# A second context tile leaves the dense second half of the expert layer: U dense, V by picked and fetched rows

## The chip, the cores and the metric

One core of a Trainium2 chip runs the whole program in one launch. The metric is the device time of one execution in microseconds (us); lower is better.

## The reference, cut to what matters

Two residual streams of 256 tokens, latents and context, pass through two layers (a mixer, then a PEER expert layer). Layer 0 mixes both streams; layer 1 needs the context only as keys and values of its mixer, after which the context is dropped.

```python
def peer_ffn(h, w_q, sub_keys, u, v):          # per 128 tokens
    q = (t @ w_q).reshape(PEER_CHUNK, PEER_HEADS, 2, PEER_KEY_HALF)
    s = jnp.einsum('thpk,hpnk->thpn', q, sub_keys)
    s_top, i_top = lax.top_k(s, PEER_TOPK)
...
    idx = jnp.take_along_axis(...)             # 8 heads x 16 = 128 experts of 16384 per token
    g = jax.nn.softmax(best_s, axis=-1)
    a = jnp.einsum('td,thkd->thk', t, u[idx])
    w = (jax.nn.gelu(a) * g)
    return jnp.einsum('thk,thkd->td', w, v[idx])
...
def odd_mixer(hl, hc, ...):                    # layer 1
    ql, kl, vl = jnp.split(hl @ w_in, ...)
    kc, vc = jnp.split(hc @ w_in[:, DIFF_QK_WIDTH:], [DIFF_QK_WIDTH], axis=-1)
    k_all, v_all = concat of latent and context
```

So each of four 128-token tiles in layer 0 (two of latents, two of context) picks 128 experts per token, and the context's result must be there before the keys and values of the context are projected in layer 1.

## The kernel before, in words

**Two ways through the expert layer.** The *dense* way multiplies a tile with all 16384 rows of U on TensorE (PE), applies GELU, multiplies by a gate table that is zero except at the tile's own 128 experts, and multiplies by all of V. Each product is three fp32r matmuls (high and low parts). The *gathered* way fetches, slot by slot, the one row per token (128 rows of 4 KB, an indirect DMA that POOL issues) and lets VectorE (DVE) do a dot product (`gather_u`) or a scaled add (`gather_v`). Both latent tiles and context tile 1 go the dense way in layer 0; context tile 0 is gathered. Layer 1 has two dense tiles (latents).

**Stages of layer 0.** Even mixer for both streams; `scores` and `route` of the context tiles, then of the latents (top-16 lists, all on DVE); `gate_table` for three tiles (DVE makes one-hots `goi`, `goj`; PE multiplies them; the table goes to DRAM). PE meanwhile runs `LEAD0` = 13 U steps ahead. Then `dense` (L600) loops 64 steps `c`: a U step (on average 1.5 units of 24 matmuls of 128x512, L634 to L636, operands `duh`, `dul`) and a V step (`w_prep`: DVE multiplies `dy` by the gates `dg`, L701, PE transposes it, L689; `v_mm`: 12 matmuls per tile, L708 to L710, operands `dvh`, `dvl`). The U steps are `LEAD0` ahead, so the last 13 steps have V alone.

**Then layer 1.** `ctx_ffn` (L885) writes the latents' norm first (`norm_T`, whose `rsqrt` is a chain of 13 small POOL instructions), then adds the context's results. `odd_mixer` (L914) projects Q of the latents (`oq`), norms the context into `oh`, and for each of 4 blocks projects K and V of both streams with one load of the weights, and runs 4 attention heads (`head`), which need K of both. `rotate` (L941) has one POOL instruction each. After the heads come the output projection, layer 1's expert layer and the final norm.

**What orders the work.** Program order and a scheduler fix a static order per engine; each engine takes its instructions in that order and waits at the head of its queue. POOL issues the indirect DMAs in the same queue in which its arithmetic stands. Row buffers (`row`, `ROWBUFS` = 4) live in the pool `vphase`, which exists only during the V steps: a fetch waits until DVE has used the row four places before.

Of the kernel before, what the change touches and what calls it, by code (L numbers as in the profile page):

```python
# [29 lines left out]
LEAD0 = 13  # L30
LEAD1 = 20
ROWBUFS = 4


def constants():
# [32 lines left out]
    c["iota"] = np.broadcast_to(np.concatenate([np.arange(128), STARTS, [1]]).astype(f32), (P, 145)).copy()  # L68
# [37 lines left out]
class Joined:  # L106
# [5 lines left out]
    def __getitem__(self, key):  # L112
        return (self.a if key[1] < 4 else self.b)[key]

# [23 lines left out]
class Builder:  # L138
# [59 lines left out]
    def setup(self, mods, *xp):  # L198
# [30 lines left out]
        self.iota, self.one = iota[:, 0:128], iota[:, 144:145]  # L229
# [236 lines left out]
    def route(self, sc, wk, ijg):  # L466
# [5 lines left out]
        va = wk.tile([P, 16, 16], F32, name="rv", bufs=2)  # L472
        ix = wk.tile([P, 16, 16], U32, name="rix", bufs=2)
# [63 lines left out]
    def gather_u(self, l, H, ijg, gp, wk):  # L537

        V, S = self.V, self.S
        idx = gp.tile([P, P], U32, name="gidx", bufs=1)  # L540
        V.scalar_tensor_tensor(idx, ijg[:, 0, :], 128.0, ijg[:, 1, :], op0=ALU.mult, op1=ALU.add)  # L541
        a = wk.tile([P, P], F32, name="pa", bufs=2)
# [5 lines left out]
        return idx  # L548

    def gather_v(self, l, idx, a, acc, gp):  # L550
        V = self.V
        for s in range(P):
            t = self.gather(gp, self.A[f"peer_v{l}"], idx, s)
# [12 lines left out]
    def gate_table(self, ijg, table, pool, ring):  # L566
# [10 lines left out]
        for t0 in range(0, P, 8):  # L577
            st = pool.tile([P, 8, P], F32, name="gst", bufs=2)
            for h in range(2):
# [12 lines left out]
                oj = pool.tile([P, 4, P], F32, name="goj", bufs=5)  # L592
# [7 lines left out]
    def dense(self, l, tables, hs, ups, yp, lead, mid, late, fin):  # L600
# [8 lines left out]
        nt = len(hs)  # L609
        uring = "c" if nt == 3 else "x"  # L610
# [18 lines left out]
        def u_unit(c, i):  # L629
            uh, ul = ut[c]  # L630
            hi, lo = hs[i]
            b = self.bank(uring)
# [9 lines left out]
        def u_step(c):  # L642
# [3 lines left out]
            for i in range((nt + 1) // 2) if c % 2 == 0 else range((nt + 1) // 2, nt):  # L646
                u_unit(c // 2, i)
# [6 lines left out]
        with self.pool("vphase") as vp:  # L654
            w = self.wide()
            pacc = [w[:, 0:512], w[:, 512:1024], self.bank("y"), self.bank("y")]
            if nt == 3:
                pacc = [self.bank("x"), self.bank("x")] + pacc[2:] + pacc[:2]
# [38 lines left out]
            def w_prep(c):  # L697
# [5 lines left out]
                if nt == 3:  # L703
                    ws[c].append(w_split("dx", lambda a: y[:, 2, a * P:(a + 1) * P], 2))
# [38 lines left out]
    def ffn(self, l, modT, h, wp, wclose, lead, extra=None, late=iter(()), finish=None):  # L743

        tables = [self.dr.tile([P, P * P], F32, name=f"table{l}{i}") for i in range(3 if extra else 2)]
        dense = [tuple(t[:, :, i * P:(i + 1) * P] for t in h) for i in range(2)]
        with self.pool("ypool") as yp:
# [7 lines left out]
            def mid():  # L755
                with self.pool("twork") as wk:
                    if extra:
                        self.gate_table(extra[1], tables[2], wk, "yx")
                    for r, table in zip(res, tables):
                        ijg = rw.tile([P, 3, P], F32, name="ijg", bufs=2)  # L760
                        self.route(r, rw, ijg)
                        self.gate_table(ijg, table, wk, "yx" if extra else "yc")
                dts.close()

            if extra:
                dense.append(extra[0])

            def fin(pacc, vp):
# [6 lines left out]
                if finish is not None:  # L775
                    finish(pacc[4:], vp)

            self.dense(l, tables, dense, ExitStack(), yp, lead, mid, late, fin)

    def run(self):  # L780
# [15 lines left out]
        with self.pool("emix") as mp, self.pool("tmp0") as self.tmp, self.pool("ework") as wk:  # L796
# [3 lines left out]
                        + [(mp, f"e{n}{s}", 1) for n in "qkvf" for s in range(2)])  # L800
# [7 lines left out]
            q, k, v, f = ([mp.tile([P, 2, 512] if n == "v" else [P, 4, 256], F32, name=f"e{n}{s}") for s in range(2)]  # L808
                          for n in "qkvf")
# [55 lines left out]
            tags = [(mp, f"e{n}{s}", 1) for n in "qkvf" for s in range(2)]  # L865
            with tc.issue_after(after):
                for m in range(3):
                    self.modulation(1, m, mod1, Tags((tags[1:] * 2)[m % 2:][:8]), "y", 1, Tags(tags[:1] * 2))
            sc1 = self.mod_scale(1, mod1, 0, 0)
            ijg1 = l0.tile([P, 3, P], F32, name="ijg1")  # L870
            self.route(sc_c[1], rw, ijg1)
# [163 lines left out]
```

## Time and profile before

| | |
|---|---|
| median of 3 runs | 2939.35 us (2938.17 to 2948.95) |
| profiled execution, its own time | 2946.36 us |
| its span on the profile | 2944.6 us |
| PE / DVE / ACT / POOL busy | 93% / 66% / 43% / 13% of the span |
| HBM traffic | 207 GB/s over the span |

The span is the time between the first and the last instruction on the profile; the execution's own time is 1.8 us more. A busy PE may still wait between stages, so the stages are read one by one. TensorE's granted clock is given as a share of its upper level (2.4 GHz).

### The profile page before, as it was taken

How to read it: one execution, taken by the hardware profiler on the slowest of the kernel's cores; microseconds unless marked ns; L12 is line 12 of the kernel's file. 1: busy time of each engine (PE TensorE's matmuls, PEld its weight loads, DVE VectorE, ACT ScalarE, POOL GpSimd, SP SyncE). 2: the span in 40 equal slices, each digit the busy share in tenths (PEclk: the TensorE clock that was granted, in tenths of full speed). 3: DMA queues.
4: the chain of work that ended last, by engine and by line, in shares of the span. 5: the costliest groups of instructions: out<-in, count | busy, mean ns of one | idle time of the engine just before them, and what ended most of it. 6: DMA issues, size and time to landing. Idle time of an engine off the chain costs nothing. (4 is left out here: it accounts for less than half of the span.)

```text
span 2944.6 us, 40707 instructions
## 1 busy us (share of the span) xinstructions
PE 2747.4 (93%) x14793; PEld 2272.7 (77%) x14793; DVE 1951.3 (66%) x3726; ACT 1266.8 (43%) x2220; POOL 391.7 (13%) x403
## 2 busy tenths in 40 slices
PE   6999987995999999999999989988898799999997
PEld 4776966885788888888788868787787688888886
DVE  3335799997778887888843445456898755555444
ACT  3334445575333333333332334344476444444443
POOL 0000000000345444545400001000000000000000
PEclk9998998997999999999999989999999899999999
DMA  6464464565989999999843423324466765666554
GB/s 244 127 221 93 157 228 133 167 182 155 360 299 340 345 342 330 343 331 329 314 157 120 155 71 125 127 65 151 155 192 202 239 234 197 212 213 208 168 158 136
DMA packets 297945, 612.83 MB, mean 208 GB/s; under 512 B 33664, under 2 KB 157328, under 8 KB 295184
## 3 DMA queue, kind: packets, MB, share of 16 engines
q1 hardware_dynamic: 260880, 475.99, 49.0%
q0 software_dynamic: 36864, 134.23, 12.4%
q8 instruction: 117, 1.92, 0.3%
q14 instruction: 84, 0.69, 0.1%
HBM read 565.04 MB, written 45.09 MB: 207 GB/s over the span
## 5 line engine op out<-in xcount | busy, mean ns | idle before, releaser
L681 DVE TENSOR_TENSOR dvl<-dv,dvh 128x1024 fp32r<-128x1024 f32 x256 | 305.4, 1221 | 231.3 <-ACT dvh L680 230.7
L634 PE MATMUL bank<-duh,h 128*128 128x512 f32 x1024 | 405.6, 399 | 7.9 <-ACT dy L640 4.8
L635 PE MATMUL bank<-dul,h 128*128 128x512 f32 x1024 | 408.0, 399 | 1.7 <-DVE dul L625 1.7
L636 PE MATMUL bank<-duh,h 128*128 128x512 f32 x1024 | 406.6, 398 | 0.0
L680 ACT ACTIVATE dvh<-dv 128x1024 fp32r<-128x1024 f32 x256 | 259.8, 1052 | 273.8 <-PE wide L710 163.6
L625 DVE TENSOR_TENSOR dul<-du,duh 128x1024 fp32r<-128x1024 f32 x256 | 310.2, 1220 | 93.5 <-ACT duh L623 92.2
L623 ACT ACTIVATE duh<-du 128x1024 fp32r<-128x1024 f32 x256 | 271.3, 1061 | 231.5 <-DMA du<-in_peer_uT 162.1
L709 PE MATMUL bank<-dvl,dwh 128*128 128x512 f32 x768 | 299.8, 391 | 0.0
L710 PE MATMUL bank<-dvh,dwl 128*128 128x512 f32 x768 | 294.2, 397 | 0.0
L708 PE MATMUL bank<-dvh,dwh 128*128 128x512 f32 x768 | 290.0, 396 | 0.0
L640 ACT ACTIVATE dy<-bank 128x256 f32<-128x256 f32 x320 | 105.0, 380 | 367.7 <-PE bank L636 349.7
L176 DVE TENSOR_TENSOR wl<-wt,wh 128x512 fp32r<-128x512 f32 x224 | 153.0, 689 | 138.0 <-ACT wh L175 136.5
L533 POOL DMA_INDIRECT row<-in_peer_u,gidx x128 | 170.4, 1331 | 551.2 <-DVE gidx L541 341.3
L634 PEld LDWEIGHTS bank<-duh,h 128*128 128x128 f32 x1024 | 193.5, 189 | 55.2 <-ACT dy L640 7.5
L635 PEld LDWEIGHTS bank<-dul,h 128*128 128x128 f32 x1024 | 193.9, 189 | 47.5 <-DVE dul L625 3.0
L636 PEld LDWEIGHTS bank<-duh,h 128*128 128x128 f32 x1024 | 193.6, 189 | 45.2
L596 PE MATMUL bank<-goj,goi 128*128 128x128 f32 x1280 | 174.1, 292 | 51.7 <-ACT goi L588 25.6
L175 ACT ACTIVATE wh<-wt 128x512 fp32r<-128x512 f32 x224 | 140.9, 631 | 183.9 <-PE bank L195 87.9
L596 PEld LDWEIGHTS bank<-goj,goi 128*128 128x128 f32 x1280 | 167.2, 205 | 63.1 <-ACT goi L588 31.5
L194 PE MATMUL bank<-h,wh 128*128 128x256 f32 x704 | 204.8, 292 | 7.1 <-ACT hf L326 6.3
L195 PE MATMUL bank<-h,wh 128*128 128x256 f32 x704 | 203.0, 289 | 1.1 <-DVE h L333 1.1
L196 PE MATMUL bank<-h,wl 128*128 128x256 f32 x704 | 202.4, 289 | 1.2 <-DVE wl L176 1.2
(261 smaller groups left out, 5655.2 us busy)
## 6 DMA issues: line engine op xcount, KB each, us to landing
du<-in_peer_uT SPq DMA_DIRECT2D x256, 512.0 KB
dv<-in_peer_v SPq DMA_DIRECT2D x256, 512.0 KB
table<-gst SPq DMA_DIRECT2D x80, 512.0 KB
dg<-table SPq DMA_DIRECT2D x320, 128.0 KB
wm<-in_w_mod SPq DMA_DIRECT2D x56, 512.0 KB
wt<-in_peer_w_q SPq DMA_DIRECT2D x96, 256.0 KB
wm<-in_w_mod SPq DMA_DIRECT2D x20, 1024.0 KB
wt<-in_odd_w_in SPq DMA_DIRECT2D x48, 256.0 KB
```

Source lines behind the costliest of these rows:

```text
L194: self.T.matmul(out, lhsT=a, rhs=b, start=k == 0 and m == 0, stop=False)
L596: T.matmul(b[:, t * P:(t + 1) * P], lhsT=oi[:, t, :], rhs=oj[:, t, :], start=True, stop=True)
L623: S.activation(th, t, AF.Copy)
L625: V.tensor_tensor(tl, t, th.bitcast(F32), ALU.subtract)
L634: T.matmul(b, lhsT=hi[:, k, :], rhs=uh[k], start=k == 0, stop=False)
L635: T.matmul(b, lhsT=hi[:, k, :], rhs=ul[k], start=False, stop=False)
L636: T.matmul(b, lhsT=lo[:, k, :], rhs=uh[k], start=False, stop=k == KT - 1)
L680: S.activation(th, v, AF.Copy)
L681: V.tensor_tensor(tl, v, th.bitcast(F32), ALU.subtract)
L708: T.matmul(b, lhsT=wh, rhs=v[0], start=first, stop=False)
L709: T.matmul(b, lhsT=wh, rhs=v[1], start=False, stop=False)
L710: T.matmul(b, lhsT=wl, rhs=v[0], start=False, stop=last)
```

## The change

- Context tile 1 keeps its dense U product, but GELU's result (`da`) goes to a DRAM table `ad` (128 tokens x 16384 experts). Its gate table, its V product and its transposes are gone.
- `pick_v`: for each of the 128 slots an indirect DMA fetches one number per token out of `ad` into a column of `pb` (a *pick*: 128 elements of 4 bytes). After every 16 picks DVE multiplies them with the gates, and 16 rows of V are fetched and added, as for tile 0.
- The experts' numbers (`gidx`) are made right after each context `route`, tile 0 first, and the row buffers live in the pool `lay0` from the even mixer on (they share their place with that mixer's context q, k, v, f). `gather_u` may so start during the routing of the other tiles.
- `LEAD0` is 16. Some buffers are smaller (`goj` 4, `rv`, `rix` 1, fewer places for the modulation's weights).
- `odd_mixer` projects Q, K and V of the latents first, with the modulations 3 and 4; then norms the context into the row buffers' place (`oh`), loads the K and V weights once more, and projects the context's K and V, with all heads in that second loop.

```diff
-LEAD0 = 13
+LEAD0 = 16
...
+    def pick_v(self, l, ad, ijg, idx, acc, gp):
...
+        flat = ad.rearrange("t (e o) -> (t e) o", o=1)
+        at = gp.tile([P, P], U32, name="gat")
+        V.tensor_scalar(at, idx, self.base, None, op0=ALU.add)
+        a = gp.tile([P, P], F32, name="pb")
         for s in range(P):
+            self.G.indirect_dma_start(out=a[:, s:s + 1], out_offset=None, in_=flat,
+                                      in_offset=bass.IndirectOffsetOnAxis(ap=at[:, s:s + 1], axis=0))
+            if s % PICK == PICK - 1:
+                c = slice(s + 1 - PICK, s + 1)
+                V.tensor_tensor(ijg[:, 2, c], a[:, c], ijg[:, 2, c], ALU.mult)
+                self.gather_v(l, idx, ijg[:, 2, :], acc, gp, range(s + 1 - PICK, s + 1))
...
+            if i == 2:
+                a = up.tile([P, UN], F32, name="da", bufs=2)
+                S.activation(a, b, AF.Gelu_apprx_tanh)
+                nc.sync.dma_start(ad[:, c * UN:(c + 1) * UN], a)
+                return
...
-                if nt == 3:
-                    ws[c].append(w_split("dx", lambda a: y[:, 2, a * P:(a + 1) * P], 2))
...
-        def ctx_ffn(pacc, vp):
+        def ctx_ffn():
             self.norm_T(1, sc1, "x", *hl)
-            self.add_ffn(1, pacc, gates[0], self.tmp.tile([P, D], F32, name="yctx"))
-            idx = self.gather_u(0, hc0, ijgc, vp, l0)
+            self.gather_u(0, hc0, ijgc, idx0, l0)
             acc = l0.tile([P, D], F32, name="gacc", tag="hc0")
-            self.gather_v(0, idx, ijgc[:, 2, :], acc, vp)
+            self.gather_v(0, idx0, ijgc[:, 2, :], acc, l0)
             self.add_ffn(0, (acc[:, :512], acc[:, 512:]), gates[0], acc)
+            acc = l0.tile([P, D], F32, name="gacc1", tag="h1c0")
+            self.pick_v(0, ad, ijg1, idx1, acc, l0)
+            self.add_ffn(1, (acc[:, :512], acc[:, 512:]), gates[0], acc)
...
         for c in range(4):
-            w = self.weight2(wp, w_in[4 + c])
-            self.project_T(kTs[1][:, c * 2:c * 2 + 2, :], w, hs[1], "x")
+            self.project_T(kTs[1][:, c * 2:c * 2 + 2, :], self.weight2(wp, w_in[4 + c]), hl, "x")
...
+            self.project(vs[1][:, :, c * 256:(c + 1) * 256], self.weight2(wp, w_in[8 + c]), hl, "x")
+            if 3 + c < 5:
+                self.modulation(1, 3 + c, modT, wk, "y", 4)
+
+        hc = [Halves(*(rows.tile([P, KT // 2, 256], F32R, name=f"oh{c}{i}", tag="row", bufs=ROWBUFS) for i in range(2)))
+              for c in range(2)]
+        self.norm_T(0, sc, "x", *hc)
+        for c in range(4):
+            self.project_T(kTs[0][:, c * 2:c * 2 + 2, :], self.weight2(wp, w_in[4 + c]), hc, "x")
+            self.project(vs[0][:, :, c * 256:(c + 1) * 256], self.weight2(wp, w_in[8 + c]), hc, "x")
```

**How the order moves.** In the changed program `gidx_4153` and `gacc` belong to context tile 0, `gidx_4343` and `gacc_13785` to context tile 1.

VectorE before, the end of the gate tables (`goi`, `goj` one-hots) and the first V step, whose first work is the multiply `dy`:

```order
L590 TENSOR_TENSOR goi<-c_iota,gsT 128x512
L593 TENSOR_TENSOR goj<-c_iota,gsT 128x512
L591 TENSOR_TENSOR goi<-goi,gsT 128x512 x3
L541 SCALAR_TENSOR_TENSOR gidx<-ijgc 128x128
L701 TENSOR_TENSOR dy<-dy,dg 128x768
L545 SCALAR_TENSOR_TENSOR row,pa<-row,hc_71 128x1024
L694 TENSOR_TENSOR dwl<-bank,dwh 128x512
```

VectorE in the changed program, first a piece of the latents' routing (`rs`, `rsm`, `rv`), then the rows around the first V step's `dy`:

```order
L458 MATCH_REPLACE rtmp<-rv,rs 128x128 x2
L524 TENSOR_TENSOR rs<-rpb,steps 128x2048
L563 SCALAR_TENSOR_TENSOR row,pa<-row,hc_71 128x1024
L542 RECIPROCAL rsm<-rsm 128x8
L563 SCALAR_TENSOR_TENSOR row,pa<-row,hc_71 128x1024
L459 MAX rv<-rtmp 128x8 x2
L563 SCALAR_TENSOR_TENSOR row,pa<-row,hc_71 128x1024
L656 TENSOR_TENSOR dul<-du,duh 128x1024
```

```order
L589 SCALAR_TENSOR_TENSOR gacc<-row,ijgc,gacc 128x1024
L623 TENSOR_TENSOR goi<-goi,gsT 128x512
L625 TENSOR_TENSOR goj<-c_iota,gsT 128x512
L623 TENSOR_TENSOR goi<-goi,gsT 128x512
L589 SCALAR_TENSOR_TENSOR gacc<-row,ijgc,gacc 128x1024 x8
L736 TENSOR_TENSOR dy<-dy,dg 128x512
L716 TENSOR_TENSOR dvl<-dv,dvh 128x1024
```

All 128 rows of `gather_u` (`row,pa`) and the first 17 of tile 0's `gather_v` (`gacc`) now stand ahead of the first `dy`; before, none did. Of the one-hots 160 stand ahead of it instead of 240, of the splits `dul` 41 instead of 29.

POOL before, tile 0's fetches and the start of the latents' norm for layer 1 (`ss`, `rs_t`, `rstd`):

```order
L533 DMA row<-in_peer_u,gidx 128x1024 x128
L533 DMA row<-in_peer_v,gidx 128x1024 x128
L312 TENSOR_SCALAR ss<-ss 128x2
L239 TENSOR_TENSOR rs_t<-rstd 128x2
L240 TENSOR_TENSOR rs_t<-rs_t,ss 128x2
L241 TENSOR_SCALAR rs_t<-rs_t 128x2
```

POOL in the changed program, from tile 0's fetches to the first picks (`pb`), and then a piece of the same norm:

```order
L548 DMA row<-in_peer_u,gidx_4153 128x1024 x128
L548 DMA row<-in_peer_v,gidx_4153 128x1024 x128
L548 DMA row<-in_peer_v,gidx_4343 128x1024 x4
L575 DMA pb<-ad,gat 128x1 x33
L548 DMA row<-in_peer_v,gidx_4343 128x1024 x2
L575 DMA pb<-ad,gat 128x1
L548 DMA row<-in_peer_v,gidx_4343 128x1024
L575 DMA pb<-ad,gat 128x1 x2
```

```order
L254 TENSOR_TENSOR rs_t<-rstd 128x2
L255 TENSOR_TENSOR rs_t<-rs_t,ss 128x2
L548 DMA row<-in_peer_v,gidx_4343 128x1024
L256 TENSOR_SCALAR rs_t<-rs_t 128x2
L257 TENSOR_TENSOR rstd<-rs_t,rstd 128x2
L548 DMA row<-in_peer_v,gidx_4343 128x1024 x11
L984 TENSOR_TENSOR oq<-oq,c_rope 128x256
L548 DMA row<-in_peer_v,gidx_4343 128x1024
L984 TENSOR_TENSOR oq<-oq,c_rope 128x256 x2
L548 DMA row<-in_peer_v,gidx_4343 128x1024
```

The 13 small instructions of the latents' norm are scattered among the picks: all 128 picks and 41 of tile 1's 128 rows stand ahead of the last of them (`rstd`). Another 46 rows stand between that and the last of the 16 rotations (`oq`, `ok`), and the last 41 behind those.

VectorE in the changed program, the end of tile 1's rows, among the splits `wl` of the weights:

```order
L191 TENSOR_TENSOR wl<-wt,wh 128x512
L589 SCALAR_TENSOR_TENSOR gacc_13785<-row,ijg_3964,gacc_13785 128x1024
L191 TENSOR_TENSOR wl<-wt,wh 128x512
L589 SCALAR_TENSOR_TENSOR gacc_13785<-row,ijg_3964,gacc_13785 128x1024 x38
L595 TENSOR_TENSOR gacc_13785<-gacc_13785,gate 128x512 x2
L596 TENSOR_TENSOR xl_12155<-xl_12155,gacc_13785 128x512 x2
L252 TENSOR_SCALAR rstd<-ss 128x2
L331 TENSOR_SCALAR xn<-xl_12153,rstd 128x1024
```

The last 38 rows stand together, with no other work between them; right behind them come the context's residual add and its norm. Before, no fetched row stood in this layer.

## Rows read from the trace of the kernel before

**Rows 1.** Busy time of each engine by stretch; columns as in its first line.
```profile
core 0: us, PE busy (x) PEld busy (x) DVE busy (x) ACT busy (x) POOL busy (x), PEclk, DMA share, GB/s
303.00:732.00 429.00, 362.96 (x2407) 317.29 (x2405) 399.04 (x1278) 237.56 (x493) 5.27 (x16) 0.94 0.53 168
732.00:1612.00 880.00, 874.03 (x3929) 711.19 (x3930) 644.59 (x751) 300.45 (x455) 347.75 (x254) 0.99 0.83 301
...
1790.00:1963.00 173.00, 170.95 (x1192) 141.79 (x1190) 84.47 (x189) 72.22 (x172) 6.28 (x8) 1.00 0.30 98
1963.00:2945.00 982.00, 910.23 (x4566) 756.54 (x4566) 617.02 (x1092) 471.60 (x738) 10.08 (x49) 0.96 0.58 187
```

**Rows 2.** PE's timeline (start, duration us): V steps without U, a projection.
```profile
1649.84 0.82 PE L689 MATMUL bank<-c_ident,dy 128*128 128x128 f32 x6
...
1658.69 0.82 PE L689 MATMUL bank<-c_ident,dy 128*128 128x128 f32 x6
...
1734.89 0.39 PE L708 MATMUL wide<-dvh,dxh 128*128 128x512 f32 x1
...
1737.39 0.39 PE L710 MATMUL wide<-dvh,dxl 128*128 128x512 f32 x1
...
1760.60 0.29 PE L195 MATMUL bank<-h,wh 128*128 128x256 f32 x1
1760.72 0.28 PE L196 MATMUL bank<-h,wl 128*128 128x256 f32 x1
```

**Rows 3.** DVE's timeline: neighbours, for the pace of each form.
```profile
600.55 1.21 DVE L625 TENSOR_TENSOR dul<-du,duh 128x1024 fp32r<-128x1024 f32 x1
601.69 0.68 DVE L591 TENSOR_TENSOR goi<-goi,gsT 128x512 f32<-128x512 f32 x1
602.29 0.28 DVE L478 CAST rixb<-rix 128x256 bf16<-128x256 uint32 x1
...
934.05 1.22 DVE L545 SCALAR_TENSOR_TENSOR row<-row,hc 128x1024 f32<-128x1024 f32 x1
935.20 0.08 DVE L545 DVE_READ_ACCUMULATOR row<-row,hc 128x1 f32 x1
...
1433.28 1.28 DVE L557 SCALAR_TENSOR_TENSOR gacc<-row,ijgc,gacc 128x1024 f32<-128x1024 f32 x1
1434.48 0.42 DVE L694 TENSOR_TENSOR dxl<-bank,dxh 128x256 fp32r<-128x256 f32 x1
```

**Rows 4.** Groups of POOL by form: count, busy us, mean ns, idle before.
```profile
L533 POOL DMA_INDIRECT row<-in_peer_v,gidx x128 | 179.8, 1405 | 174.6 <-DVE gacc L557 149.4 <-issue 12.5 <-DVE row L545 5.2
```

**Rows 5.** POOL's timeline: fetches back to back, a longer one, a norm's step.
```profile
730.35 0.94 POOL L533 DMA_INDIRECT row<-in_peer_u,gidx  x1 [0.31 <-issue]
731.59 0.94 POOL L533 DMA_INDIRECT row<-in_peer_u,gidx  x1 [0.31 <-issue]
...
1420.42 1.68 POOL L533 DMA_INDIRECT row<-in_peer_v,gidx  x1 [0.65 <-DVE gacc L557]
...
1749.49 0.19 POOL L242 TENSOR_TENSOR rstd<-rs_t,rstd 128x2 f32<-128x2 f32 x1
```

**Rows 6.** Timeline: two fetches (POOL), each with the use of its row (DVE).
```profile
1034.75 1.68 POOL L533 DMA_INDIRECT row<-in_peer_u,gidx  x1 [1.74 <-DVE row L545]
1044.35 1.23 DVE L545 SCALAR_TENSOR_TENSOR row<-row,hc 128x1024 f32<-128x1024 f32 x1 [3.61 <-DMA row<-in_peer_u,gidx]
1430.40 0.94 POOL L533 DMA_INDIRECT row<-in_peer_v,gidx  x1 [1.45 <-DVE gacc L557]
1435.35 1.29 DVE L557 SCALAR_TENSOR_TENSOR gacc<-row,ijgc,gacc 128x1024 f32<-128x1024 f32 x1 [0.45 <-DMA row<-in_peer_v,gidx]
```

**Rows 7.** Timeline after the last V matmul: last residual add, norm, first projection.
```profile
1742.48 1.28 DVE L564 TENSOR_TENSOR xl<-xl,yadd 128x512 f32<-128x512 f32 x2
1756.34 0.58 PE L194 MATMUL bank<-h,wh 128*128 128x256 f32 x1 [0.84 <-ACT hf L326]
```

**Rows 8.** Busy time of L270 (modulations) in the heads' stretch: PE, PEld.
```profile
1790.00:1963.00 173.00, 14.34 (x64) 2.25 (x64) 1.00 0.30 98
```

More of the change, by code (lines that the diff above doesn't have):

```diff
@@ L29 @@
 UN = 512
-LEAD0 = 13
+LEAD0 = 16
 LEAD1 = 20
 ROWBUFS = 4
+PICK = 16
 def constants():
@@ L113, in __getitem__, with __init__ @@
         return (self.a if key[1] < 4 else self.b)[key]
+class Halves:
+    def __init__(self, a, b):
+        self.a, self.b = a, b
+    def __getitem__(self, key):
+        p, k, n = key
+        if isinstance(k, slice):
+            return (self.a if k.start < 4 else self.b)[p, :, n]
+        return (self.a if k < 4 else self.b)[p, k % 4, n]
 class Slots:
@@ L535, in gather, with experts, gather_u @@
         return t
[L537 removed]
+    def experts(self, ijg, pool, name):
+        idx = pool.tile([P, P], U32, name=name)
+        self.V.scalar_tensor_tensor(idx, ijg[:, 0, :], 128.0, ijg[:, 1, :], op0=ALU.mult, op1=ALU.add)
+        return idx
+    def gather_u(self, l, H, ijg, idx, gp):
         V, S = self.V, self.S
[L540 to L542 removed]
+        a = gp.tile([P, P], F32, name="pa")
         for s in range(P):
@@ L645, in u_step @@
                 return
-            for i in range((nt + 1) // 2) if c % 2 == 0 else range((nt + 1) // 2, nt):
+            n = len(hs)
+            for i in range((n + 1) // 2) if c % 2 == 0 else range((n + 1) // 2, n):
                 u_unit(c // 2, i)
@@ L741, in dense, with ffn @@
             fin(pacc, vp)
-    def ffn(self, l, modT, h, wp, wclose, lead, extra=None, late=iter(()), finish=None):
-        tables = [self.dr.tile([P, P * P], F32, name=f"table{l}{i}") for i in range(3 if extra else 2)]
+    def ffn(self, l, modT, h, wp, wclose, lead, extra=None, late=iter(()), finish=None, ad=None):
+        tables = [self.dr.tile([P, P * P], F32, name=f"table{l}{i}") for i in range(2)]
         dense = [tuple(t[:, :, i * P:(i + 1) * P] for t in h) for i in range(2)]
@@ L775, in fin @@
                 if finish is not None:
-                    finish(pacc[4:], vp)
-            self.dense(l, tables, dense, ExitStack(), yp, lead, mid, late, fin)
+                    finish()
+            self.dense(l, tables, dense, ExitStack(), yp, lead, mid, late, fin, ad)
     def run(self):
@@ L799, in run @@
             tags = Tags([(p, f"h{c}", 1) for p in (hcp, self.pers) for c in range(2)]
-                        + [(mp, f"e{n}{s}", 1) for n in "qkvf" for s in range(2)])
+                        + [(l0, "row", ROWBUFS)] * 4 + [(mp, f"e{n}1", 1) for n in "qkvf"])
             mods = [self.mod_steps(0, m, mod0, tags, "c", 1, n=(4, 2)) for m in range(2)]
@@ L807, in run @@
             sc_mix = self.mod_scale(0, mod0, 0, 0)
-            q, k, v, f = ([mp.tile([P, 2, 512] if n == "v" else [P, 4, 256], F32, name=f"e{n}{s}") for s in range(2)]
-                          for n in "qkvf")
+            q, k, v, f = ([(mp if s else l0).tile([P, 2, 512] if n == "v" else [P, 4, 256], F32, name=f"e{n}{s}",
+                                                  tag=f"e{n}1" if s else "row", bufs=1 if s else ROWBUFS)
+                           for s in range(2)] for n in "qkvf")
             h = hc, hl = [[p.tile([P, KT, 256], F32R, name=f"h{c}") for c in range(2)] for p in (hcp, self.pers)]
@@ L912, in run, with odd_mixer @@
         right.close()
-    def odd_mixer(self, cp, mp, wk, wp, sc, modT, hl):
+    def odd_mixer(self, cp, mp, wk, wp, sc, modT, hl, rows):
         nc, A, V, S, G, T = self.nc, self.A, self.V, self.S, self.G, self.T
-        hs = [mp.tile([P, KT, 256], F32R, name=f"oh{c}") for c in range(2)], hl
         rope = self.const("rope", cp)
```

59 lines of the change are left out of this document (26 added, 33 removed).

## The prediction

> **What bounds the kernel now.** I read the busy times by stretch first, because the share of the whole span (PE 93%) hides stages with other limits. Four stretches matter [rows 1]. From 303 to 732 us (routing and gate tables) VectorE is busy 399 of 429 us and PE 363: VectorE sets this stretch. From 732 to 1612 us (U and V steps together) PE is busy 874 of 880 us, VectorE 645: PE sets it, and all 256 row fetches of context tile 0 lie here, hidden beside it. From 1790 to 1963 us (odd mixer's K, V and heads) PE is busy 171 of 173 us. The last 982 us are layer 1 and are not changed. Then I read the paces, which are the distances between starts and not the durations, because neighbours overlap: one 128x512 matmul each 0.227 us (11 steps in 2.50 us), one 128x256 matmul each 0.12 us, one V step of three tiles each 8.85 us [rows 2].
>
> **What PE loses.** A three-tile V step is 36 x 0.227 = 8.17 us of matmuls and 0.68 us of six transposes. Two tiles leave 24 x 0.227 + 0.45 = 5.90 us. A U step (36 matmuls on average) stays at 8.17 us. The stretch with both had 51 of each: 51 x (8.17 + 8.85) = 868 of the 880 us, so 12 us are its start. With three more steps of lead it has 48 U steps and 47 V steps up to the last U product: 48 x 8.17 + 47 x 5.90 + 12 = 681 us. That is 199 us less. Another 17 V steps, 100 us, follow it. The splits and `dy` work that go with the third tile leave VectorE here; it was not the limit, so this is worth nothing. The write of `ad` stands in SP's queue 32 times and waits for GELU; `du` is fetched three buffers ahead, so I cost it at nothing.
>
> **What VectorE gains ahead of it.** By the order shown, all 128 dot products of `gather_u` and 17 adds of `gather_v` stand before the first V step, 12 more U splits (the longer lead), and 80 one-hots fewer. Paces [rows 3]: dot product 1.15, add 1.20, split 1.14, one-hot 0.60 us. Sum: 147 + 20 + 14 - 48 = +133 us, on the engine that sets the stretch and had only 30 us idle. The low end is that the idle time takes them in, +103 us; the high end adds some 30 us in which VectorE waits for a row in its queue (nothing behind it can pass), +163 us. I take +133: the first V step's `dy` moves from 732 to 865 us. The lead's 3 extra U steps (25 us of PE) run under it. So the last U product ends at 865 + 681 = 1546 us (before: 1612), and the V steps could end at 1646 us (before: 1738). These two parts together are the gain: 92 us.
>
> **What POOL gets.** The first pick needs the whole of `ad`, so it waits for 1546 us and some 3 us for GELU and the write. Behind that wait, in POOL's queue, stand the latents' norm for layer 1 and the 16 rotations; VectorE waits in its own queue for each group of 16 picks, with V steps' work behind it. By the order, 128 picks and 37 rows (4 of the 41 are ahead) must pass before the norm is finished. Its matmuls can't start earlier, so the 100 us of V steps are no full cover any more.
> - *A pick or a fetch on POOL.* No row shows a pick. It has as many indices as a row fetch (128), so I take the row fetch for it: back to back 0.94 us and 0.30 us to the next, 1.24 in all; the longer kind 1.68 + 0.30 = 1.98 us [rows 5]. The mean of the V fetches was 1.41 us [rows 4], 1.71 with the step, while VectorE was busy 73% of its stretch [rows 1]. Beside the tail VectorE's work is some 45% (34 splits, 34 smaller operations and the rows in 250 us): 1.24 + 0.47 x 45/73 = 1.5 us. 165 x 1.5 = 248 us; ends 205 and 327.
> - *The other 87 rows.* Four buffers: a buffer turns once per landing, use and restart. From a fetch's start to its row's use I read 4.95 us at best and 9.60 us in a crowded stretch [rows 6]; the use takes 1.20 us [rows 3], the restart 0.65 [rows 5]. So one row each (4.95 + 1.85)/4 = 1.70 to (9.60 + 1.85)/4 = 2.86 us. The 46 rows among the rotations run beside the weights' loads: 2.1 us each, 97 us. The last 41 have the DMA nearly alone: 1.75 us each, 72 us. Ends for all 87: 148 and 249 us.
>
> The Trainium skill ("DMA: Bandwidth & Descriptors", the section on the anatomy of a DMA on the gpsimd path) gives 2.0 us plus bytes/436 GB/s for one such transfer, 3.2 us for these 512 KB. By that a buffer would turn in (0.94 + 3.2 + 1.85)/4 = 1.5 us, an estimate, and the sum would be 39 us smaller. The shortest time that I found here, 4.95 us, is above it, so the sum goes by the trace.
>
> The 12 latent projections with the modulations and rotations (12 x 48 x 0.12 + 17 + 4 = 90 us of PE) fit beside the 46 rows. The last 41 rows have nothing beside them: by the order VectorE has 38 adds in one run there, and PE has no work that doesn't need the context. So the last add is at 1546 + 3 + 248 + 97 + 72 = 1966 us.
>
> **The context, last.** The residual add (2.6 us) and the norm to the first projection (1743.8 to 1756.3, 12.6 us [rows 7]) are now exposed: 15 us; before, they lay beside the Q projections. Then K and V of the context and all heads: of 173 us [rows 1] the latents' half of K and V (8 x 48 x 0.12 = 46 us) and two modulations (14.3 us [rows 8] and some 2.5 of transposes) are already done, which leaves 110 us. The weights' second load and 32 more splits stand beside it (ACT had 72, VectorE 84 us of work in the 173): nothing, if the loads come in time. The heads end at 1966 + 15 + 110 = 2091 us; before, at 1963.
>
> **The sum.** +128 us on the profiled execution: 2946.4 + 128 = 3074 us. It was 7 us above the median of the runs, so I forecast 3067 us, 4.3% slower. A measurement of this kernel can tell some 0.5% from no change, 15 us.
>
> With all low ends together (first V step at 835, 1.24 us per pick, 1.70 per row) the heads end at 835 + 681 + 3 + 205 + 148 + 125 = 1997 us, which is still 34 us later than before, 2973 us. With the high ends of POOL and rows it is 3067 + 79 + 80 = 3226 us.
>
> **The rivals.**
> - *A pick is cheap for POOL* (faster). The fetch's 0.94 us may be for its 512 KB and not for its 128 indices; a pick moves 512 bytes. POOL's small instructions take 0.19 us and 0.08 to the next [rows 5]. At 0.27 us the 128 picks are 35 us, and with 37 rows at 1.5 the 248 us become 90: 3067 - 158 = 2909 us, 1% faster. It turns the sign from about 0.50 us per pick downwards. For it: nothing in the trace separates indices from bytes. Against it: a fetch starts moving while POOL still works, and its time has two levels, 0.94 and 1.68, for the same bytes, so it is set on POOL and not by the transfer. The Trainium skill, in the section named above, calls descriptor generation "small, variable" beside about 2 us of completion, which is this rival's rule; the 0.94 us rows don't agree, but they are all of 4 KB pieces. Chance 0.11.
> - *POOL at its long level throughout* (slower still). If each pick meets a VectorE operation that holds it up, as the 1.68 us fetch did, 165 x 1.98 = 327 us: 3146 us. For it: VectorE has rows and splits in every gap. Against: the mean in a busier stretch was 1.41 us. Chance 0.14.
> - *Even*: picks near 0.5 us, or all low ends and a shorter context stage. 2925 to 2955 us. Chance 0.06.
> - *The forecast*, picks and rows at the paces read, 2960 to 3130 us. Chance 0.69.
>
> Slower by more than 0.5% is the forecast and the second rival, 0.83; within 0.5% is 0.06; faster is 0.11. The range 2960 to 3170 us takes in the forecast, its unknown ends and the slow rival, and leaves out the cheap pick, the even case and the far high end.
>
> **What would show it.** In the changed profile: `dy` first at about 865 us; the last `h1c` matmul at about 1546; POOL's `pb` group x128 at a mean of 0.9 to 1.7 us; the latents' `xn` transposes wait for POOL's chain until about 1800 us; PE idle some 100 us there and some 60 us before the `oh` projections; the last `gacc` row at about 1966. A `pb` mean under 0.5 us, or a first `dy` before 800 us, would make the forecast wrong.

## The result, and the profile after

The changed kernel takes **3120.06 us** (median of 4 runs, 3118.03 to 3129.62); the kernel before, in the same comparison, 2941.1 us. The ratio is 1.061, its 95% interval 1.058 to 1.064. The forecast was 3067 us, slower by 4.3%: sign and range held, and the size fell 53 us short. The profiled execution took 3129.6 us on a span of 3127.6. Runs of one kernel lie up to 22 us apart, so differences of that size between medians are read together with the traces.

Busy time by stretch of the changed kernel, columns as in its first line; the stretches are cut where the prediction's steps end (first `dy`, last U product, picks, latents' projections, last run of rows, context, rest):

```profile
core 0: us, PE busy (x) PEld busy (x) DVE busy (x) ACT busy (x) POOL busy (x), PEclk, DMA share, GB/s
303.00:882.00 579.00, 395.43 (x2359) 335.94 (x2358) 531.52 (x1473) 215.04 (x411) 237.63 (x162) 0.85 0.78 260
882.00:1540.00 658.00, 655.72 (x2928) 533.85 (x2929) 420.31 (x407) 254.32 (x346) 153.51 (x111) 0.99 0.77 269
1544.00:1783.00 239.00, 112.93 (x470) 87.58 (x469) 100.58 (x106) 47.38 (x59) 167.58 (x164) 0.73 0.46 147
1794.00:1933.00 139.00, 109.26 (x681) 91.00 (x681) 104.86 (x145) 41.98 (x74) 67.20 (x64) 0.85 0.91 331
1945.00:2021.00 76.00, 0.00 (x0) 0.00 (x0) 51.03 (x41) 0.63 (x1) 45.23 (x35) 0.50 0.81 273
2022.00:2145.00 123.00, 110.99 (x728) 93.93 (x728) 80.33 (x177) 67.15 (x168) 2.51 (x13) 0.93 0.21 69
2145.00:3127.00 982.00, 908.83 (x4566) 755.70 (x4566) 617.97 (x1092) 471.74 (x737) 10.07 (x49) 0.96 0.58 187
```

Against [rows 1]: the first stretch, which VectorE sets, grew from 429 to 579 us; the one with U and V together, which PE sets, shrank from 880 to 658; then come 480 us of a kind that the kernel before did not have, in which PE is busy for under half the time and, from 1945 to 2021 us, not once. Layer 1 behind the heads is 982 us in both.

POOL's groups by form (count, busy us, mean ns, idle before it and what ended that):

```profile
L548 POOL DMA_INDIRECT row<-in_peer_v,gidx x256 | 357.8, 1398 | 395.5 <-DVE gacc L589 314.7 <-issue 23.4 <-DVE modT L295 19.8
...
L575 POOL DMA_INDIRECT pb<-ad,gat x128 | 131.9, 1030 | 306.8 <-DMA ad<-da 268.6 <-issue 37.0 <-DMA pb<-ad,gat 1.2
```

POOL's timeline at the first picks:

```profile
1544.03 0.95 POOL L575 DMA_INDIRECT pb<-ad,gat  x1 [268.55 <-DMA ad<-da]
1545.28 0.95 POOL L575 DMA_INDIRECT pb<-ad,gat  x1 [0.30 <-issue]
1546.54 0.95 POOL L575 DMA_INDIRECT pb<-ad,gat  x1 [0.30 <-issue]
```

A pick of 512 bytes holds POOL for 0.95 us and 0.30 to the next, as a row of 512 KB does in [rows 5]: the cheap pick did not happen. The means, 1.03 and 1.40 us, hold longer ones too, and these go with VectorE's work: of the 384 row fetches in this trace, the 54 with no VectorE instruction beside their first 0.94 us took 0.94 on the mean and 0.96 at most; the 260 that had one all that while took 1.56. For picks it is 0.94 (59 of them) and 1.18 (24). No run changed that work alone. The first pick waited 269 us for the last piece of `ad`; context tile 0 had long been done.

What was waited for from 1795 to 1945 us, beside the latents' projections (total us, times, longest):

```profile
PE bank L336 <- DVE xn L331: 86.2, 1, 86.2
...
ACT wh L190 <- DMA wt<-in_odd_w_in: 44.4, 22, 5.9
POOL row L548 <- DVE gacc L589: 42.0, 29, 4.3
ACT mrow L288 <- PE bank L285: 31.7, 4, 11.6
POOL row L548 <- DVE modT L295: 19.8, 4, 8.0
DVE wl L191 <- ACT wh L190: 19.2, 7, 7.8
...
DVE gacc L589 <- DMA row<-in_peer_v,gidx: 8.1, 4, 3.9
```

The first line is the wait for the latents' norm, which stood behind the picks. The rest is the part that the forecast had too small. VectorE waited only 8 us for rows that had not landed. POOL waited 42 us for VectorE's adds and 20 for its `modT`, and VectorE waited for the weights' splits. One place of that kind, on four engines in order of PE, ACT, DVE, POOL (start, duration):

```profile
1877.23 1.05 PE L285 MATMUL bank<-wm,silu 128*32 128x512 f32 x4 [1.50 <-DMA wm<-in_w_mod]
```
```profile
1878.39 0.60 ACT L288 ACTIVATE mrow<-bank 128x512 f32<-128x512 f32 x1 [11.58 <-PE bank L285]
```
```profile
1879.54 0.69 DVE L191 TENSOR_TENSOR wl<-wt,wh 128x512 fp32r<-128x512 f32 x1 [5.78 <-ACT wh L190]
1880.19 0.19 DVE L293 TENSOR_REDUCE mt<-bank 128x8 f32<-128x32 f32 x1
1880.30 1.28 DVE L589 SCALAR_TENSOR_TENSOR gacc<-row,ijg,gacc 128x1024 f32<-128x1024 f32 x1
1881.49 0.16 DVE L295 TENSOR_TENSOR modT<-mt,cols 128x8 f32<-128x8 f32 x1
```
```profile
1881.85 1.22 POOL L548 DMA_INDIRECT row<-in_peer_v,gidx  x1 [6.88 <-DVE modT L295]
```

A modulation's matmuls wait for their weights; ACT waits for them with `mrow`, and behind it in ACT's queue stands a weight's `wh`; VectorE waits for that `wh` with `wl`, and behind it stands the add of a row that is there already; POOL waits for the buffer. Here the rows are passengers of the projections; that they hold the projections up as well shows under half rows.

### The profile page after: what moved, and what is told of

It reads as the page before. It is cut to its first block, busy times and chain, and to the rows that moved or that the text cites. A ratio compares the mean times of both kernels' runs of the same rounds, so it can differ in the third digit from the quotient of the medians.

```text
span 3127.6 us, 38786 instructions
## 1 busy us (share of the span) xinstructions
PE 2570.1 (82%) x13638; PEld 2114.5 (68%) x13638; DVE 2047.8 (65%) x3751; ACT 1221.1 (39%) x2057; POOL 708.7 (23%) x659
## 3 DMA queue, kind: packets, MB, share of 16 engines
q8 instruction: 107, 1.75, 0.2%
## 4 chain that ended last, share of the span: by engine, by line
PE 54%; DVE 14%; DMA 13%; issue 10%; POOL 5%; ACT 2%; another core or an unknown queue 2%; SPq 0%; POOLq 0%; ACTq 0%; DVEq 0%
PE bank L667 7%; PE bank L665 7%; PE bank L666 7%; PE wide L743 3%; PE wide L742 3%; PE wide L741 3%; PE bank L741 3%; PE bank L742 3%; PE bank L743 3%; DVE row L563 3%; PE bank L209 3%; PE bank L211 3%; PE bank L210 3%; DMA table<-gst 3%; DMA wm<-in_w_mod 2%
## 5 line engine op out<-in xcount | busy, mean ns | idle before, releaser
L665 PE MATMUL bank<-duh,h 128*128 128x512 f32 x1024 | 406.2, 399 | 68.4 <-ACT duh L654 62.3
L548 POOL DMA_INDIRECT row<-in_peer_v,gidx x256 | 357.8, 1398 | 395.5 <-DVE gacc L589 314.7
L665 PEld LDWEIGHTS bank<-duh,h 128*128 128x128 f32 x1024 | 193.9, 190 | 115.9 <-ACT duh L654 62.8
L191 DVE TENSOR_TENSOR wl<-wt,wh 128x512 fp32r<-128x512 f32 x256 | 174.8, 688 | 137.6 <-ACT wh L190 135.9
L741 PE MATMUL wide<-dvh,dwh 128*128 128x512 f32 x512 | 213.8, 418 | 49.0 <-ACT dvh L715 38.8
L190 ACT ACTIVATE wh<-wt 128x512 fp32r<-128x512 f32 x256 | 160.6, 631 | 216.4 <-PE bank L210 94.4
L548 POOL DMA_INDIRECT row<-in_peer_u,gidx x128 | 175.4, 1371 | 234.3 <-DVE row L563 110.2
L589 DVE SCALAR_TENSOR_TENSOR gacc<-row,ijg,gacc 128x1024 f32<-128x1024 f32 x127 | 166.4, 1310 | 79.9 <-DMA row<-in_peer_v,gidx 79.0
L254 POOL TENSOR_TENSOR rs_t<-rstd 128x2 f32<-128x2 f32 (+1 forms) x27 | 6.8, 251 | 932.1 <-DVE rstd L252 930.9
L742 PE MATMUL wide<-dvl,dwh 128*128 128x512 f32 x512 | 207.0, 404 | 1.5 <-issue 1.1
L743 PE MATMUL wide<-dvh,dwl 128*128 128x512 f32 x512 | 203.9, 398 | 0.5 <-issue 0.3
```

What stands on the lines that cost most here:

```text
L548: self.G.indirect_dma_start(out=t, out_offset=None, in_=table, in_offset=bass.IndirectOffsetOnAxis(ap=idx[:, s:s + 1], axis=0))
L741: T.matmul(b, lhsT=wh, rhs=v[0], start=first, stop=False)
L742: T.matmul(b, lhsT=wh, rhs=v[1], start=False, stop=False)
L743: T.matmul(b, lhsT=wl, rhs=v[0], start=False, stop=last)
```

## The experiments

The edits start from the changed kernel unless another is named. Medians of 4 runs each; every ratio is to runs of the kernel before on the same chip.

| kernel | median us | ratio, 95% interval |
|---|---|---|
| changed | 3120.1 | 1.061, 1.058 to 1.064 |
| U rows late | 3054.9 | 1.038, 1.036 to 1.040 |
| latents' norm on VectorE | 3094.2 | 1.051, 1.049 to 1.053 |
| every pick twice | 3244.2 | 1.102, 1.100 to 1.104 |
| no picks | 2981.2 | 1.013, 1.011 to 1.014 |
| half rows | 3108.0 | 1.057, 1.053 to 1.060 |
| U rows late, norm on VectorE | 3073.2 | 1.042, 1.039 to 1.045 |
| the same, six buffers | 3014.0 | 1.022, 1.020 to 1.025 |
| U rows split, six buffers | 3007.7 | 1.021, 1.019 to 1.022 |
| the same, norm on VectorE | 2991.7 | 1.015, 1.013 to 1.016 |
| the same, modulations late | 2978.4 | 1.010, 1.008 to 1.012 |
| modulations late alone | 3118.0 | 1.057, 1.053 to 1.060 |

### U rows late

```diff
-            self.gather_u(0, hc0, ijgc, idx0, l0)
+            with tc.issue_after(self.first):      # dy of V step 0
+                self.gather_u(0, hc0, ijgc, idx0, l0)
```

> The changed kernel with one part undone: the fetches and dot products of context tile 0's U rows wait for the first V step (the multiply dy of step 0), as they did in the kernel before; the rest is as changed. In the changed kernel dy comes first at 882 us, with all 128 dot products and 17 adds ahead of it. Theory (VectorE sets the stretch ahead of the first V step, and the rows there delay it one for one): dy first at 735 to 750 us, the last U product at 1395 to 1425 us, and everything behind it moves by the same, less what tile 0's rows of V now spill behind the U steps (by the order about 31 of them still stand among the picks, each some 1.5 us, 45 us): total 3120 - 130 + 45 = 3035 us, 3000 to 3060. Rival (the rows only fill VectorE's idle time there, and PE's own work sets the first V step): dy at 850 us or later, and total 3120 us or more, since tile 0's rows come later.

The total is in the theory's range. The first `dy` came even earlier (`dy` by form: shortest, median and longest ns, then first and last start in us):

```profile
L736 DVE TENSOR_TENSOR dy<-dy,dg x128: 677/686/760, 706.0 to 2904.4; 128x512 f32<-128x512 f32 x128
```

706 us and not 882: 176 us for 145 rows moved, 1.21 us each, VectorE's own pace for them. The last U product moved by about as much, 1540 to 1371 us. But tile 0's rows of V, which had been done at 1274 us, now ended at 1652, and the last row of tile 1 came only 80 us earlier, at 1939. What the early rows cost VectorE ahead, the late ones cost POOL behind.

### The latents' norm on VectorE

```diff
-            self.norm_T(1, sc1, "x", *hl)
+            self.norm_T(1, sc1, "x", *hl, G=V)    # its 13 small instructions
```

> The changed kernel; the 13 small instructions of the latents' norm for layer 1 run on VectorE and not in POOL's queue behind the picks, so the latents' projections need not wait for 128 picks and 41 rows. Theory (the last row of context tile 1 sets the end, and PE's idle time beside the picks costs only what it pushes onto the rows): xn of the latents at about 1700 us and not 1794, PE idle less by 90 us between 1540 and 1800, but idle longer ahead of the context's projections; the last row still comes at 1960 to 2010 us (2020 in the changed kernel), because the same 128 picks and 128 rows go through POOL; the gain is what the crowd with the weights' loads cost, 10 to 60 us: total 3060 to 3110 us. Rival (the blocked norm itself is the loss): total falls by the whole idle time of PE there, some 150 us, to about 2970 us.

As the theory said: `xn` at 1692 us, 102 earlier, last row at 1983, and 26 us gained, not 150. PE's 86 us of waiting for the norm were not the loss; the rows set the end. The edit frees the norm alone, though. The first rotation still stands in POOL's queue behind the last pick, so the projections could not be done before it:

```profile
1766.17 0.94 POOL L575 DMA_INDIRECT pb<-ad,gat  x1 [0.30 <-issue]
1767.15 2.82 POOL L984 TENSOR_TENSOR oq<-oq,c_rope 128x256 f32<-128x256 f32 x3
```

No run moved norm and rotations together. Busy time of the stretches behind the picks (columns as above), with the projections and without:

```profile
1767.00:1840.00 73.00, 48.80 (x248) 29.32 (x247) 53.43 (x74) 14.27 (x24) 40.33 (x40) 0.81 0.93 340
1840.00:1910.00 70.00, 0.00 (x0) 0.00 (x0) 47.45 (x40) 0.00 (x0) 46.91 (x38) 0.50 0.79 265
1910.00:1982.00 72.00, 0.00 (x0) 0.00 (x0) 48.88 (x38) 0.00 (x0) 44.58 (x37) 0.50 0.82 277
```

Of the adds (DVE), 20 lie in the first, 74 in the 142 us behind it: 3.65 us per row beside the projections, 1.92 alone.

### Every pick twice, and none

```diff
+            self.G.indirect_dma_start(out=a2[:, s:s + 1], out_offset=None, in_=flat, ...)
```

> The changed kernel with every pick issued twice (the second copy goes to a buffer that nobody reads): 128 more indirect DMAs of 512 bytes in POOL's queue, nothing else. Theory (a pick costs POOL as much as a row fetch, by its 128 indices and not by its bytes, and lies on the path): 128 x 1.24 to 1.5 us = 159 to 192 us more, total 3280 to 3310 us; the group of second copies has a mean near 1.03 us. Rival (picks are cheap, or hidden by the V steps and the row buffers that the rows wait for anyway): 0 to 50 us more, total 3120 to 3170 us.

124 us more, 0.97 us per added pick (107 us between the two profiled executions): on the path, neither cheap nor hidden, but below the theory's 159 to 192 us too. Part of the added time was covered by waits that POOL had anyway: it waited 291 us for VectorE's adds of V rows, and 315 in the changed kernel. The two groups of picks among POOL's:

```profile
L578 POOL DMA_INDIRECT pc<-ad,gat x128 | 135.3, 1057 | 38.7 <-issue 34.5 <-DMA pb<-ad,gat 2.1 <-DMA pc<-ad,gat 1.8
L576 POOL DMA_INDIRECT pb<-ad,gat x128 | 133.1, 1040 | 307.2 <-DMA ad<-da 268.7 <-issue 36.1 <-DMA pc<-ad,gat 1.5
```

```diff
-            self.G.indirect_dma_start(out=a[:, s:s + 1], ...)
...
-                V.tensor_tensor(ijg[:, 2, c], a[:, c], ijg[:, 2, c], ALU.mult)
```

> The changed kernel without its 128 picks: tile 1's rows of V are weighted by the gates alone, so GELU's values (the U result of context tile 1) are left out of its output; they are still computed and written to DRAM. Without them tile 1's rows need not wait for the last U product, so this takes away the picks' time on POOL and the wait ahead of them together. Theory (picks and their place in POOL's queue are the loss): the latents' norm is done at about 1665 us, the last row at 1810 to 1890 us, the heads end 122 us later, total 2905 to 2985 us. Rival (the rows set the end by themselves: 128 rows at the 3.3 us each that 46 of them took beside the latents' projections): the last row at about 1970 us, total near 3065 us.

2981 us, at the edge of the theory's range; last row at 1874 us, 146 earlier. But the wait ahead of the picks did not go with them. Tile 1's first add, and the fetch that needs its buffer:

```profile
1541.56 0.75 DVE L581 TENSOR_SCALAR gacc<-row,ijg 128x1024 f32<-128x1024 f32 x1 [2.59 <-PE bank L660]
1542.58 1.86 POOL L548 DMA_INDIRECT row<-in_peer_v,gidx  x1 [265.70 <-DVE gacc L581]
```

The sum of tile 1's rows (`gacc1`) lies in the place of `h1c0`, the activations that the U products of this tile read until 1541 us. So POOL still waited 266 us for the last U product, picks or not, and the expectation's premise was wrong. The 139 us, of the 179 that the change lost, are the picks' time alone, 1.09 us each. Without them it is still 1.3% slower than before. That the late first V step and the context's place at the end outweigh the shorter dense part fits this, but the run does not separate them from that wait.

### Half rows

```diff
-            t = self.gather(gp, self.A[f"peer_v{l}"], idx, s)
+            self.G.indirect_dma_start(out=t[:, :512], in_=half, ...)   # "e (h d) -> (e h) d", index x 2
```

> The changed kernel; each of context tile 1's 128 fetches of V brings only the first half of its row (128 pieces of 2 KB and not of 4 KB), and VectorE adds that half to both halves of the sum, so its work stays at one add of 128x1024. The second half of those V rows is left out of the result. Question: what made tile 1's rows beside the latents' projections cost 3.3 us each where the forecast had 2.1. Theory (the DMA engines, 0.9 busy there with the weights' loads): half the bytes bring that pace to about 2.1 us, and the rows alone at the end from 1.87 to 1.4 to 1.6 us; the last row at 1930 to 1965 us and not 2019, total 3030 to 3075 us; POOL's time for one fetch stays at 0.94 us back to back. Rival (VectorE's splits of the weights, and POOL, hold the rows): the pace stays at 3 us or more, the last row at 2005 to 2025 us, total 3105 to 3125 us.

The pace is the rival's; the last row, at 1988 us, lies between the two. Busy time of its stretches beside the projections and behind them, columns as above:

```profile
1796.00:1912.00 116.00, 100.75 (x678) 84.08 (x679) 96.96 (x139) 42.50 (x75) 64.35 (x56) 0.91 0.81 275
1912.00:1989.00 77.00, 3.61 (x29) 3.19 (x27) 65.33 (x57) 3.12 (x5) 57.42 (x45) 0.54 0.60 178
```

38 adds in 116 us are 3.05 us per row, as in the changed kernel (45 in 139, 3.1), though the DMA share fell from 0.91 to 0.81 and each row has half the bytes. So a row's own bytes do not set that pace. But the projections went faster: from the latents' `xn` to their last rotation they took 115 us and not 137. What went is most of ACT's wait for the modulations' matmuls, 31.7 us in the changed kernel:

```profile
ACT mrow L288 <- PE bank L285: 5.8, 3, 5.1
```

So the rows also hold the projections up, beside which the weights are loaded. Whether their bytes do it or their number is open, since in this order 37 fetches stand in that stretch and not 46. The median fell by 12 us only; the profiled execution, the fastest of its four, is 30 below that of the changed kernel. Alone, 48 in 77 us are 1.60, no longer held by the landing but by POOL, whose timeline there has no gap but the 0.30 us to the next issue:

```profile
1949.86 1.21 POOL L598 DMA_INDIRECT row<-in_peer_v,two  x1 [0.30 <-issue]
1951.37 1.13 POOL L598 DMA_INDIRECT row<-in_peer_v,two  x1 [0.30 <-issue]
1952.80 1.29 POOL L598 DMA_INDIRECT row<-in_peer_v,two  x1 [0.30 <-issue]
```

### Both edits, and six buffers

> Both of the earlier edits together: context tile 0's U rows wait for the first V step, and the latents' norm runs on VectorE. With the U rows late, the last U product came at 1371 us, and PE then waited 294 us for that norm. Theory (the last row of context tile 1 sets the end; the norm's place decides only beside what the weights' loads run): the rows now have the DMA alone at 1.9 us each and not 3.1 beside the loads, some 50 rows, so 30 to 60 us less than with late U rows alone, total 2995 to 3025 us, and PE waits as long, only later. Rival (PE's wait for the norm is the loss): it falls by 200 us or more, total 2850 us.

Neither: 3073 us, 18 more than with late U rows alone (28 between the profiled executions). The picks took 243 us and not 230, and the last 17 rows of tile 0 behind them another 80 us, from 1633 to 1714, beside the projections' last part. The theory wanted loads and rows apart; they were not. Its `xn` came at 1546 us, but the first rotation again only behind the last pick, at 1634, and the projections ended at 1731. What the theory had not counted is that rows of either tile, put between a projection's splits and rotations, take that long.

```diff
-        t = gp.tile([P, D], F32, name="row", bufs=ROWBUFS)
+        n = s % (ROWBUFS + 2) - ROWBUFS           # for tile 1's V rows
+        tag = ("h1c1", "hc0")[n] if n >= 0 else None
+        t = gp.tile([P, D], F32, name="row", tag=tag, bufs=1 if tag else ROWBUFS)
```

> Both edits, and two more buffers for context tile 1's rows of V, six in all, in places that are free by then (the low half of tile 1's activations and the place of tile 0's sum). Theory (with four buffers a row alone costs its landing, use and restart over four, 1.9 us): with six it comes down to what POOL (1.24 us) and VectorE (1.3 us) allow or the DMA engines (0.8 busy at 1.9 us, so 1.5 us when full): 1.5 to 1.6 us each for 127 rows, 40 to 50 us less than with both edits alone, total 2950 to 2985 us. Rival (the DMA engines or the landing are the limit already, and more rows in flight only land later): 0 to 10 us less.

59 us less than with four. The total misses its range because the base did. Busy time while tile 1's rows run alone, columns as above, first with four buffers, then with six:

```profile
1735.00:1966.00 231.00, 0.00 (x0) 0.00 (x0) 154.29 (x120) 0.00 (x0) 144.36 (x120) 0.50 0.81 274
```
```profile
1712.00:1907.00 195.00, 4.90 (x12) 3.04 (x12) 165.27 (x136) 0.47 (x1) 153.30 (x126) 0.50 0.94 341
```

231 us for 120 rows are 1.93 each, 195 for 126 fetches 1.55, with the DMA engines at 0.94. The turn of a buffer set the pace with four, as the prediction had it. With six POOL has no gap left:

```profile
1830.60 1.03 POOL L548 DMA_INDIRECT row<-in_peer_v,gidx  x1 [0.30 <-issue]
1831.93 1.62 POOL L548 DMA_INDIRECT row<-in_peer_v,gidx  x1 [0.31 <-issue]
```

Its 153 us of work and 126 times 0.30 us make 191 of the 195. That the DMA engines would be the next limit is not shown: half rows came to the same pace with them at 0.60.

### U rows split

```diff
+            with self.tc.issue_after(self.first) if s >= 48 else ExitStack():
                 t = self.gather(gp, self.A[f"peer_u{l}"], idx, s)
```

> The changed kernel with the U rows of context tile 0 split: 48 fetches and dot products stay ahead of the first V step, 80 wait for it; and six buffers for tile 1's rows of V. The latents' norm stays on POOL. With all U rows late, 208 row fetches went through between the first V step (706 us) and the last U product (1371 us), 48 too few to finish tile 0; with all early, POOL waited 269 us for the U result. Theory (48 early rows at 1.2 us of VectorE each are the balance): first dy at 760 to 785 us, last U product at 1425 to 1450 us, tile 0's V rows done by then; 128 picks and some 57 rows in 185 x 1.35 = 250 us, to about 1690 us; the last 71 rows at 1.6 to 2.5 us, last row 1800 to 1865 us, total 2905 to 2970 us. Rival (rows spill again, or VectorE's queue holds the V steps behind them): last U product after 1480 us or tile 0's rows done after 1500 us, total 2990 us or more.

The first half is the theory's: `dy` at 771 us, last U product at 1432, tile 0's last row at 1446 and the first pick at 1445, so POOL's wait for `ad` is down to 3 us. The second is not: the picks ended at 1712 us, the last row came at 1889, 24 us beyond the theory's latest, and the total is 38 above its range. Beside the projections (158 us from `xn` to the last rotation) 63 adds took 2.5 us each, although six buffers gave 1.55 alone.

> As split_u, and the latents' norm on VectorE, so that their projections run beside the picks, when the DMA engines are half idle. Theory: the same up to the last U product (1425 to 1450 us); the picks and 50 rows 10 to 20 us longer, since rows and picks now share VectorE and POOL with the projections; but no row waits behind a weight's split after about 1720 us: the last 45 to 78 rows at 1.55 us, last row 1785 to 1840 us, total 2890 to 2945 us. Rival (the projections hold rows and picks back wherever they stand, as they did with both earlier edits together, where the picks took 243 us and not 230, and 17 rows behind them 80 us): no better than split_u, or up to 25 us worse.

16 us better than split_u, and 47 above the range: the picks, with 46 rows and the projections beside them, took 1446 to 1719 us, and the first rotation stood behind them once more, at 1725. The last row came at 1887.

### Modulations late

```diff
-            if 3 + c < 5:
-                self.modulation(1, 3 + c, modT, wk, "y", 4)
...
+        for m in (3, 4):                          # behind the context's loop
+            self.modulation(1, m, modT, wk, "y", 4)
```

> The changed kernel with modulations 3 and 4 taken out of the loop of the latents' projections and put behind the context's loop; nothing left out. With half the bytes per row, tile 1's rows beside the latents' projections came no faster (42 in 122 us), so their own bytes do not set that pace. Theory now (the order does: those rows stand in VectorE's queue between the splits of the weights, and a split waits for ACT, which in that stretch waits 32 us for the modulations' matmuls and 44 us for weights): without the modulations the stretch from the latents' norm to their last rotation takes 105 to 115 us and not 138, the last row comes at 1985 to 2000 us and not 2019, and the modulations cost 10 to 17 us of PE later: total 3095 to 3115 us. Rival (each row's own landing and use over four buffers, 3.3 us, whatever stands between): the stretch keeps 130 us or more, the last row comes at 2010 us or later, total 3120 to 3140 us.

Busy time beside the projections and behind them, columns as above:

```profile
1792.00:1910.00 118.00, 92.00 (x589) 84.70 (x589) 98.86 (x130) 38.66 (x68) 68.89 (x61) 0.85 0.87 304
1910.00:2001.00 91.00, 7.15 (x35) 6.95 (x35) 65.64 (x60) 4.67 (x8) 51.79 (x43) 0.53 0.82 281
```

118 us and not 139 for 43 rows, and the last row at 1999 us, although the first pick was 10 us later. That is near the theory's upper end (115 us for norm to last rotation was the limit; it is 117), against the rival's 130. The median shows next to nothing of it: 3118 us, 3 above the range. In the profiled executions the last row comes 20 us earlier and the end 10, so half of it comes back behind the last row, where the modulations now stand.

> The fastest version so far with tile 1 picked (48 early U rows, six buffers, the latents' norm on VectorE: 2992 us) and the modulations 3 and 4 behind the context's loop. There the latents' projections run beside the picks, 1620 to 1820 us, and hold back rows and picks in the same order. Theory: 10 to 30 us less ahead of the last row (1880 us there), 10 to 17 us more behind it: 2970 to 2995 us. Rival (picks on POOL set that stretch, 270 us for 128 picks and 46 rows, whatever runs beside them): the last row at 1875 to 1885 us, total 2995 to 3010 us. In no case below the kernel before, 2941 to 2947 us.

2978 us, last row at 1873: 13 us less, inside the theory's range (between the profiled executions the last row is 14 us earlier, the end 3). It is the fastest version found that has the picks, and it is 1.0% slower than the kernel before. None beats it.

## Why the prediction was right, and where its size was off

- **First V step**: 882 us, forecast 865. VectorE's work ahead of it grew by 132.5 us (531.5 against 399.0), forecast 133. Its idle time grew too, from 30 to 47.5 us, inside the bound of +30 given for waits on rows. Late U rows confirm that each row there delays the V steps by its own 1.2 us.
- **U and V together**: 658 us, forecast 681; the last U product at 1540, forecast 1546. The two misses nearly cancel, and not by luck alone: while the first `dy` was late, PE ran further ahead. It had 29 U units done when the first `dy` came (232 matmuls of L665 by 882 us, 8 each) and not the 24 of the lead: 5 x 24 x 0.227 = 27 us that the sum put behind it. The V steps ended at 1709 us, where the prediction had 1646 as possible; they were not on the path.
- **Picks on POOL**: 1544 us to the latents' `xn` at 1794, 250 us; forecast 1549 to 1797, 248. That a pick holds POOL as a row fetch does was right. The common price of 1.5 us was right as a mean only, which is partly luck: 128 picks at 1.03 + 0.30 us are 170 us, and the other 80 went into 37 rows and the norm's steps, some 2.2 per row. The cheap pick and the long level are both out. One argument against the cheap pick, that a fetch starts moving while POOL still works, is not borne out: in the lone fetches of the traces the first packet starts 0.69 us or more after the instruction's end. The Trainium skill ("DMA: Bandwidth & Descriptors", anatomy of one DMA on the gpsimd path) calls descriptor generation "small, variable"; here 128 of them, 4 bytes each, cost POOL 0.94 us at the least, the same as 128 of 4 KB.
- **The 46 rows beside the latents' projections**: this is the term that was mis-sized. The prediction read 2.1 us per row from a buffer's turn, 97 us, and held that 90 us of PE work "fit beside" them. It was the other way round: the projections took 139 us (PE busy 109, at a granted clock of 0.85, waiting for weights and for ACT), and the rows, in fixed places of VectorE's and POOL's queues, went along. Half the bytes left the pace per row as it was but shortened the projections by 22 us, and taking the modulations out by 20. In both, ACT's wait for the modulations' matmuls is gone or nearly, so some 20 of the 42 us hang on the modulations. How the rest divides between the DMA engines' crowd, the clock and the order was not taken apart: no run kept the loads and freed the rows.
- **The last run of rows**: 88 us from 1933 to 2021 (2.0 us each for 44), forecast 72 (1.75 for 41). The mechanism held, as six buffers show; the landing was longer than the best one of [rows 6]: from a fetch's start to its row's use the last 40 rows took 5.76 us (median; 4.70 at best) and not 4.95, and (5.76 + 1.85)/4 is 1.90. (The 4.95 is not the shortest of the kernel before either; its trace has one of 4.41.) By the page of the Trainium skill named above ("DMA: Bandwidth & Descriptors", the same section) it would have been 1.5 us with four buffers, an estimate; no run with four buffers and whole rows came under 1.87 (38 adds in the 71 us from 1950).
- **Context last**: last add 2021 us to heads' end 2144.5, 124 us; forecast 125. The rest was equal, 983 against 982.

The sum: heads' end 2144.5 against 2091, 53 us, which is 42 us beside the projections and 16 in the last run, less small change. The cause of the loss stands as forecast: a stage that only POOL and VectorE can do, row by row, lies between the last U product and PE's first work on the context, and the 72 us by which that product came earlier (1612 to 1540) are far from paying for it.

## What to carry to other kernels

When a gather moves behind a dense stage, count its instructions on the engine that issues them, by number and not by bytes: 128 numbers hold POOL, at the least, as long as 128 rows do. Small work that is put between the steps of a larger stage on an in-order queue takes that stage's pace, and can slow it; price it by the stage's own chain of waits and not by its buffers alone. When an experiment is to take a wait away, look for a second one behind it (a place that two buffers share, work left in the same queue). A resource freed on one engine (PE here) gives nothing while the next stage waits for another; the balance of early and late rows won 112 us, together with two more buffers, without changing that.

## What the runs showed of the hardware that was not expected

- POOL's time for an indirect DMA did not follow the bytes of its 128 indices: 0.94 us at the least for 4 bytes, 2 KB and 4 KB each. It was longer beside VectorE's work (0.94 and 1.56 us on the mean for rows of the changed kernel).
- In the last run of rows PE had no matmul and its granted clock stood at 0.50, the lower level (1.2 GHz); it read 0.93 over the stretch behind it, which took no longer than forecast.
- With six rows in flight the DMA engines were 0.94 busy at 341 GB/s, with four 0.81 at 274. POOL, issuing back to back, set the pace with six.
